# Square sums of five norms and the forget gate's running sum: fp32r products of two halves in place of fp32 products

## The chip, the cores and the metric

The kernel runs on one core of one Trainium2 chip. The metric is the time of the whole program on the device, in microseconds (us). Five engines work side by side, each through its own list of instructions in the order of the program: TensorE (PE, matrix products; PEld are its weight loads), VectorE (DVE), ScalarE (ACT), GpSimd (POOL) and SyncE (SP, which here only starts transfers). An instruction waits until what it reads has been written and what it overwrites has been read; whatever stands behind it on the same engine waits with it.

## The reference, cut to what matters

A decoder trunk of two layers on 256 tokens of width 1024. Every layer is a SwiGLU feed-forward (ffn), a token mixer (attention A in layer 0, attention B with forget gates in layer 1) and a second ffn. An RMS norm stands ahead of each of them and ahead of the shared keys and values:

```python
def rms_norm(x, g):
    xf = x.astype(jnp.float32)
    y = xf * lax.rsqrt(jnp.mean(xf * xf, axis=-1, keepdims=True) + EPS)
    return (y * g.astype(jnp.float32)).astype(x.dtype)
...
    log_f = jax.nn.log_sigmoid((h @ fgate_w + fgate_b).astype(jnp.float32))
    F = jnp.cumsum(log_f, axis=1)
```

## The kernel before

Activations lie transposed: `x` is eight tiles (chunks k = 0 to 7) of 128 features x 256 tokens. Every large product is split in three fp32r products: weight and activation are each kept as a high half (`wh`, `HH`, `hidh`) and a low half (`wl`, `HL`, `hidl`), and `mm3` forms high x high, low x high and high x low.

**Weights.** They come as 348 pieces `raw` (mostly 128 x 1024 fp32), six buffers deep. For each piece ACT makes `wh` (a cast, `cp_part`) and DVE makes `wl` (`raw` minus `wh`, `sub_part`), always in the order of the pieces. When `wl` of piece p has been made, SP starts the load of piece p+6 into the buffer that comes free. In an ffn's up-projection a unit j (256 gate and 256 up columns) takes four pieces, two chunks k each: the first piece serves k = 0 and 1 of the unit, the second k = 2 and 3, and so on, with 24 products for a piece.

**Order.** The class `InOrder` wraps each engine and keeps an estimated time `t` for it. Between the instructions that are written out, `bg`, `fill_act` and `fill_dve` put casts, subtractions and `ada_block`s (a 128 x 1024 multiply-and-sum on DVE that makes modulation columns) where these estimates leave room. A product whose second operand is F32 counts four times in PE's estimate. Inside `plain(f)` nothing is filled in. So each instruction that is added, and each product whose type changes, moves later fillings.

**Norms.** `x_update(n, ...)` (L438) runs once per chunk n: DVE adds the gated result to `x[n]`, ACT writes `HH` (x times the scale) and the squares `sq`, and the deferred `second()` writes `HL` on DVE and adds `sq` into `acc` (on POOL for n < 7 in the two attention outputs, else on DVE). `rstd_of` (L457) sums `acc` over the 128 partitions with one fp32 product against `ones` (1/1024 everywhere) into `psn`, ACT takes the reciprocal root `r0`, and three DVE instructions on `ra` refine it. The norm is taken late: the first products of the next stage run on the unnormed `HH`, `HL` (tiles `lp`, or `lg` and `lu`), and `psn` stands among them, after 24 of them in `late_pairs` and after 36 in `ffn(..., "late", ...)`. `MakeH` then makes the normed halves chunk by chunk: `ht` (DVE), `HH` (ACT), `HL` (DVE). There are five such norms: after ffn 0 and before attention A; after attention A and before ffn(0,1); before the shared keys and values; before attention B; after attention B and before ffn(1,1). The first norm of the program takes its squares another way (`sqs`, `parts`).

**Forget gate.** `lf` (16 x 256) is turned by two PE transposes into `plf`, ACT copies it to `lft`, and two fp32 products with the triangle `ub` (inside the constants tile `tri`) give the running sum `pFk`.

Of the kernel before, what the change touches and what calls it, by code (L numbers as in the profile page):

```python
# [10 lines left out]
F32 = mybir.dt.float32  # L11
F32R = mybir.dt.float32r
BF16 = mybir.dt.bfloat16
AF = mybir.ActivationFunctionType
ALU = mybir.AluOpType
PSUM = bass.MemoryType.PSUM

P = 128
D = 1024
S = 256  # L20
NC = D // P
HD = 64
AH = 8
BH = 16
# [80 lines left out]
def trunk(ctx, tc, a, out):  # L105
# [3 lines left out]
    act = InOrder(tc, nc.scalar, 0.13, 1 / 1200)  # L109
    dve = InOrder(tc, nc.vector, 0.08, 1 / 960)  # L110
    sp = InOrder(tc, nc.sync, 0.0, 1 / 704)
    cp_ = ctx.enter_context(tc.tile_pool(name="cp", bufs=1))
# [3 lines left out]
    kp = ctx.enter_context(tc.tile_pool(name="kp", bufs=2))  # L116
# [8 lines left out]
    def abank(name):  # L125
        return pp.tile([P, 512], F32, tag="ta", name=name)
# [4 lines left out]
    mm = pe.matmul  # L131

    def plain(f, *args):

        r = []
        act.plainly(lambda: dve.plainly(lambda: r.append(f(*args))))
        return r[0]
# [7 lines left out]
    for k in range(0, NC, 4):  # L145
        sp.dma_start(xx[:, k:k + 4], a["x"][:, k:k + 4])
    x = [xx[:, k] for k in range(NC)]
    ones = cp_.tile([P, P], F32, name="ones")
    dve.memset(ones, 1.0 / D)
    eps = cp_.tile([P, 1], F32, name="eps")  # L150
    dve.memset(eps, EPS)
# [13 lines left out]
    def table(func):  # L165
        act.preload_act_table(func)
# [66 lines left out]
    def need(*ms):  # L233
        while ada_done[0] < 2 * max(ada_at[m] for m in ms):
            credit[0] -= 1
            dve.plainly(ada_block)
# [163 lines left out]
    def run_laters():  # L400
        for e in list(laters):
            e[0] -= 1
            if e[0] <= 0:
                laters.remove(e)
                e[1]()

    def later(n, f):
        laters.append([n, f])
# [18 lines left out]
    acc = [None]  # L427

    def shift_cols(nxt):
# [2 lines left out]
        act.copy(HH[:, :, S:SX], shb)  # L432
        dve.tensor_tensor(HL[:, :, S:SX], shb, HH[:, :, S:SX].bitcast(F32), op=ALU.subtract)

    def x_update(n, ps, gate, nxt, acc_eng):

        dve.scalar_tensor_tensor(x[n], ps, gate[:, n:n + 1], x[n], op0=ALU.mult, op1=ALU.add)
        hh, hl = hn[n]  # L440
        A = mods[nxt[0]][1]
        act.activation(hh, x[n], AF.Copy, scale=A[:, n:n + 1])
        sq = kp.tile([P, S], F32, tag="sq", name=f"sq{n}")
        act.activation(sq, x[n], AF.Square)

        def second():
            dve.scalar_tensor_tensor(hl, x[n], A[:, n:n + 1], hh.bitcast(F32),
                                     op0=ALU.mult, op1=ALU.subtract)
            if n == 0:
                acc[0] = sq  # L450
            else:
                t = kp.tile([P, S], F32, tag="acc", name="acc", bufs=1) if n == 1 else acc[0]
                (acc_eng if n < NC - 1 else dve).tensor_tensor(t, acc[0], sq, op=ALU.add)
                acc[0] = t
        return second

    def rstd_of(then=None, parts=None):  # L457
        ps = abank("psn")[:, :S]
        parts = parts or [acc[0]]
        for i, p in enumerate(parts):  # L460
            mm(ps, ones, p, start=i == 0, stop=i == len(parts) - 1)
        r0 = kp.tile([P, S], F32, tag="r0", name="r0", bufs=1)
        act.activation(r0, ps, AF.Abs_reciprocal_sqrt, bias=eps)
        if then is not None:
            table(then)
        ra = kp.tile([P, S], F32, tag="ra", name="ra", bufs=1)
        dve.scalar_tensor_tensor(ra, ps, eps, r0, op0=ALU.add, op1=ALU.mult)
        dve.scalar_tensor_tensor(ra, ra, -0.5, r0, op0=ALU.mult, op1=ALU.mult)
        dve.scalar_tensor_tensor(r0, ra, 1.5, r0, op0=ALU.add, op1=ALU.mult)
        return r0  # L470
# [93 lines left out]
    def ffn(l, i, kind, m, nxt, at=2):  # L564
# [120 lines left out]
        for n in range(NC):  # L685
# [22 lines left out]
            def upd(n=n, po=po):  # L708
                f = x_update(n, po, mods[gate][1], nxt, dve)
                later(1, f)  # L710
# [167 lines left out]
    def v_proj(src, dst):  # L878

        for nh in range(2):  # L880
            banks = [mmbank(f"pv{t}") for t in range(2)]
            for kh in range(2):
                blk = take(src)
                for kk in range(4):
                    k = kh * 4 + kk
                    wh, wl = blk(kk * 512, 512)
                    hh, hl = hn[k]
                    for t in range(2):
                        ts = slice(t * P, t * P + P)
                        mm(banks[t], hh[:, ts], wh, start=k == 0, stop=False)  # L890
                        mm(banks[t], hh[:, ts], wl, start=False, stop=False)
                        mm(banks[t], hl[:, ts], wh, start=False, stop=k == NC - 1)
                        work(256)
                    if k == NC - 1:
                        for t in range(2):
                            act.copy(dst[t][nh], banks[t])
                    yield kk, 4
# [39 lines left out]
    for k in range(0, NC, 2):  # L937
        sq = kp.tile([P, 512], F32, tag="w512a" if k % 4 else "w512b", name=f"sqs{k}")
        act.activation(sq, xx[:, k:k + 2].rearrange("p a b -> p (a b)"), AF.Square)
        sq4.append(sq)  # L940
        if k % 4:
            i = k // 4
# [4 lines left out]
    ada_block()  # L947
    ada_block()
    rstd = rstd_of(None, [sq4[i][:, h * S:(h + 1) * S] for i in (0, 2) for h in range(2)])
    warm(6)  # L950
    pb = sbank("pb")[:AH, :UW]
# [5 lines left out]
    late = {}  # L957

    def constants():
        o = P + 2 * S  # L960
        raw = ap_.tile([P, 2, D], F32, tag="ada", name="misc").rearrange("p a b -> p (a b)")
        sp.dma_start(raw[:, :a["misc"].shape[1]], a["misc"])
        tri = cp_.tile([P, o], F32R, name="tri")
        late["mask"] = tri[:, 2 * P:P + S].bitcast(F32)
        late["ident"], late["ub"] = tri[:, :P].bitcast(F32), tri[:, P + S:].bitcast(F32)
        base = o

        def bias():
            act.copy(tri, raw[:, :base])
            table_ = kp.tile([AH, UW], F32, tag="w512b", name="table_")  # L970
            dve.tensor_copy(table_, ut)
            udram = tc.dram_tile([AH, UW], F32, name="udram")
            nc.gpsimd.dma_start(udram, table_)
            skew = tc.dram_tile([AH, P, UW], F32, name="skew")
            for hd in range(AH):
                nc.gpsimd.dma_start(skew[hd], bass.AP(udram.tensor, udram.offset + hd * UW, [[0, P], [1, UW]]))
            late["skew"] = skew

            ls = small[:, :2]
            lj = kp.tile([P, HD], F32, tag="w512a", name="lj")  # L980
            for i in range(2):
                q = o + 2 * i * HD
                dve.tensor_tensor_reduce(lj, raw[:, q:q + HD], raw[:, q + HD:q + 2 * HD], 1.0, 0.0,
                                         ALU.mult, ALU.add, accum_out=ls[:, i:i + 1])
            act.activation(ls, ls, AF.Exp)
            nlam = small[:, 2:3]
            dve.scalar_tensor_tensor(nlam, ls[:, 1:2], -LAMBDA_INIT, ls[:, 0:1],
                                     op0=ALU.add, op1=ALU.subtract)
            subg = small[:, 8:9]
            dve.tensor_scalar_mul(subg, vecs[:, V_SUB:V_SUB + 1], 1.0 - LAMBDA_INIT)  # L990
            late["nlam"], late["subg"] = nlam, subg
        later(10, bias)
# [6 lines left out]
    ident, mask, ub, skew, nlam, subg = (  # L999
        late[n] for n in ("ident", "mask", "ub", "skew", "nlam", "subg"))  # L1000
# [176 lines left out]
    op, rest = attention_a()  # L1177
# [40 lines left out]
    for i, (kk, n) in enumerate(v_proj("wkv", vb)):  # L1218
        if mh:
            mh.go()  # L1220
        run_laters()
        if i == 5:
            plf = abank("plf")
            for t in range(2):
                pe.transpose(plf[:, t * BH:(t + 1) * BH], lf[:, t * P:(t + 1) * P], ident[:BH, :BH])
            lft = kp.tile([P, 2 * BH], F32, tag="lft", name="lft", bufs=1)
            act.copy(lft, plf[:, :2 * BH])
        if i == 7:
            pFk = abank("pFk")
            mm(pFk[:BH, P:S], lft[:, BH:], ub[:, :P], start=True, stop=False, skip_group_check=True)  # L1230
            mm(pFk[:BH, :S], lft[:, :BH], ub, start=False, stop=True, skip_group_check=True)
            fk = kp.tile([BH, S], F32, tag="w512b", name="fk")
            act.activation(fk, pFk[:BH, :S], AF.Copy, scale=-1.0)

            fdram = tc.dram_tile([BH, P + S], F32, name="fdram")
            nc.gpsimd.dma_start(fdram[:, :P], fk[:, :P])
            nc.gpsimd.dma_start(fdram[:, P:], fk)
        if i == 8:
            need(*nm_)
            table(AF.Silu)  # L1240
            mh = MakeH(rstd, nm_)
            mh.go()
# [147 lines left out]
    op, rest = attention_b()  # L1390
# [130 lines left out]
```

## Time and profile before

| | |
|---|---|
| median of 3 runs | 968.13 us (968.04 to 970.2) |
| the profiled execution | 968.25 us, its span 966.5 us |
| PE busy | 957.2 us (99%) |
| DVE busy | 819.6 us (85%) |
| ACT busy | 558.7 us (58%) |
| granted TensorE clock | 0.999 of full |

The span is what the profile's rows cover; the time of the same execution is 1.75 us longer. In a timeline a row reads: start, duration, engine, line, operation, output<-inputs, shape, and in brackets how long the engine had been idle and what ended that. Matmuls are pipelined: a row's duration is longer than the step to the next row's start, and the step is what a product costs. Since the wrapper issues every instruction, nearly all rows carry its line, L100, and are told apart by tiles.

### The profile page before, as it was taken

What the parts mean: (1) busy time and instruction counts of PE and PEld (TensorE: products, weight loads), DVE (VectorE), ACT (ScalarE), POOL (GpSimd) and SP (SyncE); (2) the same over time, 40 slices, a digit from 0 to 9 for tenths busy, and PEclk for the clock granted to TensorE, in tenths of its full rate; (3) what the DMA queues carried; (4) which work ended last, traced back from release to release, by engine and by line L of the source; (5) the groups of instructions that cost most, each with busy time, mean ns of one, the idle gap of its engine ahead of it and who ended that gap; (6) DMA issues with size and microseconds to landing.
All of it is one profiled execution on the core that took longest, in us unless ns stands there. A gap on an engine that the chain in (4) does not pass through costs nothing.

```text
span 966.5 us, 20431 instructions
## 1 busy us (share of the span) xinstructions
PE 957.2 (99%) x8076; PEld 931.4 (96%) x8076; DVE 819.6 (85%) x1364; ACT 558.7 (58%) x911; POOL 68.6 (7%) x110
## 2 busy tenths in 40 slices
PE   9999999999999999999999999999999999999997
PEld 7999999998999999999997999999998899999997
DVE  6989978889999999878889989989988799555575
ACT  6575545576787745455576545445568676554432
POOL 0000200000112000000000000000053014300000
PEclk9999999999999999999999999999999999999999
DMA  9998999968767699888959799988895337977651
GB/s 357 414 369 293 346 385 332 327 216 282 288 206 261 204 364 387 309 291 311 327 178 379 292 340 340 353 302 317 318 313 158 115 120 223 269 163 258 189 150 44
DMA packets 69518, 267.87 MB, mean 277 GB/s; under 512 B 9429, under 2 KB 10270, under 8 KB 59311
## 3 DMA queue, kind: packets, MB, share of 16 engines
q1 hardware_dynamic: 66060, 259.35, 76.3%
q0 software_dynamic: 3072, 6.92, 2.5%
q8 instruction: 63, 1.03, 0.4%
q10 hardware_dynamic: 290, 0.32, 0.1%
q14 instruction: 33, 0.26, 0.1%
HBM read 264.41 MB, written 2.66 MB: 276 GB/s over the span
## 4 chain that ended last, share of the span: by engine, by line
PE 97%; DVE 1%; ACT 1%; issue 0%; POOL 0%; ACTq 0%
PE po L100 25%; PE pg L100 21%; PE pu L100 21%; PE pv L100 5%; PE pf L100 5%; PE lp L100 4%; PE pqk L100 3%; PE pw L100 3%; PE lq L100 1%; PE lu L100 1%; PE lg L100 1%; PE pk L100 1%; PE wb L100 1%; PE sb L100 1%; PE s L100 1%; DVE ada L100 1%
## 5 line engine op out<-in xcount | busy, mean ns | idle before, releaser
L100 ACT CAST wh<-raw 128x1024 fp32r<-128x1024 f32 (+1 forms) x360 | 347.8, 975 | 221.5 <-PE pu L100 77.2
L100 DVE TENSOR_TENSOR wl<-raw,wh 128x1024 fp32r<-128x1024 f32 (+1 forms) x360 | 400.6, 1132 | 70.2 <-ACT sg L100 20.6
L100 DVE CUSTOM_DVE_ANT_0 ada<-ada,cact,vecs 128x1024 f32<-128x1024 f32 x160 | 203.2, 1281 | 0.4 <-DMA ada<-in_ada 0.4
L100 PE MATMUL pg<-HH,wl 128*128 128x256 f32 x608 | 168.2, 277 | 0.0
L100 PE MATMUL pu<-HH,wh 128*128 128x256 f32 x608 | 168.1, 277 | 0.0
L100 PE MATMUL pg<-HL,wh 128*128 128x256 f32 x608 | 168.1, 277 | 0.0
L100 PE MATMUL pu<-HH,wl 128*128 128x256 f32 x608 | 168.1, 276 | 0.0
L100 PE MATMUL pu<-HL,wh 128*128 128x256 f32 x608 | 168.1, 276 | 0.0
L100 PE MATMUL pg<-HH,wh 128*128 128x256 f32 x608 | 168.1, 276 | 0.0
L100 PE MATMUL po<-hidh,wh 128*128 128x256 f32 x528 | 145.9, 276 | 0.0
L100 PE MATMUL po<-hidl,wh 128*128 128x256 f32 x528 | 145.9, 276 | 0.0
L100 PE MATMUL po<-hidh,wl 128*128 128x256 f32 x528 | 145.9, 276 | 0.0
L100 PEld LDWEIGHTS pg<-HH,wl 128*128 128x128 f32 x608 | 114.2, 188 | 0.1
L100 PEld LDWEIGHTS pg<-HH,wh 128*128 128x128 f32 x608 | 114.2, 188 | 0.0
L100 PEld LDWEIGHTS pu<-HH,wh 128*128 128x128 f32 x608 | 114.2, 188 | 0.0
L100 PEld LDWEIGHTS pg<-HL,wh 128*128 128x128 f32 x608 | 114.2, 188 | 0.0
L100 PEld LDWEIGHTS pu<-HL,wh 128*128 128x128 f32 x608 | 114.2, 188 | 0.0
L100 PEld LDWEIGHTS pu<-HH,wl 128*128 128x128 f32 x608 | 114.2, 188 | 0.0
L100 PEld LDWEIGHTS po<-hidh,wh 128*128 128x128 f32 x528 | 99.2, 188 | 0.0
L100 PEld LDWEIGHTS po<-hidh,wl 128*128 128x128 f32 x528 | 99.1, 188 | 0.0
L100 PEld LDWEIGHTS po<-hidl,wh 128*128 128x128 f32 x528 | 99.1, 188 | 0.0
L100 ACT CAST hidh<-hf 128x512 fp32r<-128x512 f32 x44 | 27.3, 621 | 42.0 <-DVE hf L100 42.0
(228 smaller groups left out, 1857.6 us busy)
## 6 DMA issues: line engine op xcount, KB each, us to landing
raw<-in_win SPq DMA_DIRECT2D x176, 512.0 KB, 6.8
ada<-in_ada SPq DMA_DIRECT2D x79, 1024.0 KB, 7.5
raw<-in_wout SPq DMA_DIRECT2D x48, 384.0 KB, 5.5
raw<-in_wout SPq DMA_DIRECT2D x48, 320.0 KB, 5.3
raw<-in_wqk SPq DMA_DIRECT2D x16, 512.0 KB, 5.1
raw<-in_wo SPq DMA_DIRECT2D x16, 512.0 KB, 5.4
raw<-in_wlast SPq DMA_DIRECT2D x16, 512.0 KB, 4.0
raw<-in_wv SPq DMA_DIRECT2D x8, 512.0 KB, 7.0
```

Of the source, the lines that this page charges most:

```text
L100: return self.tc.keep_in_program_order(f(*args, **kw))
```

## The change

In each of the five norms the finished sum `acc` is split, right after its last addition: ACT copies it to fp32r (`acc_sq` in the order's rows, a buffer of the tag that the squares use) and DVE subtracts that copy from `acc` (`acc_ht`, a buffer of the tag that `ht` uses). Two fp32r products with the same `ones` replace the one fp32 product. The first norm keeps its fp32 products. For the forget gate, `lft` becomes fp32r with twice the columns: ACT writes the high half, one more DVE instruction the low half, and the products with `ub` are done for both.

```diff
-    ones = cp_.tile([P, P], F32, name="ones")
+    ones_r = cp_.tile([P, P], F32R, name="ones")
+    ones = ones_r.bitcast(F32)
...
+    def halves(t):
+
+        h, l = (kp.tile([P, S], F32R, tag=tag, name=f"acc_{tag}") for tag in ("sq", "ht"))
+        act.copy(h, t)
+        dve.tensor_tensor(l, t, h.bitcast(F32), op=ALU.subtract)
+        return h, l
...
-                acc[0] = t
+                acc[0] = t if n < NC - 1 else plain(halves, t)
...
-        parts = parts or [acc[0]]
+        w = ones if parts else ones_r
+        parts = parts or acc[0]
         for i, p in enumerate(parts):
-            mm(ps, ones, p, start=i == 0, stop=i == len(parts) - 1)
+            mm(ps, w, p, start=i == 0, stop=i == len(parts) - 1)
...
-            lft = kp.tile([P, 2 * BH], F32, tag="lft", name="lft", bufs=1)
-            act.copy(lft, plf[:, :2 * BH])
+            lft = kp.tile([P, 4 * BH], F32R, tag="lft", name="lft", bufs=1)
+            act.copy(lft[:, :2 * BH], plf[:, :2 * BH])
+            dve.tensor_tensor(lft[:, 2 * BH:], plf[:, :2 * BH], lft[:, :2 * BH].bitcast(F32), op=ALU.subtract)
...
-            mm(pFk[:BH, P:S], lft[:, BH:], ub[:, :P], start=True, stop=False, skip_group_check=True)
-            mm(pFk[:BH, :S], lft[:, :BH], ub, start=False, stop=True, skip_group_check=True)
+            for o in (BH, 3 * BH):
+                mm(pFk[:BH, P:S], lft[:, o:o + BH], ub[:, :P], start=o == BH, stop=False, skip_group_check=True)
+            for o in (0, 2 * BH):
+                mm(pFk[:BH, :S], lft[:, o:o + BH], ub, start=False, stop=o > 0, skip_group_check=True)
```

The order of the instructions moves as well. The first place is the norm between attention A and ffn(0,1), on DVE. Before, from the last addition into `acc` (the three `wl` in one row are pieces 110 to 112 of the weights, the single `wl` is piece 113):

```order
L100 TENSOR_TENSOR acc<-acc,sq_4010 128x256
L100 TENSOR_TENSOR wl<-raw,wh 128x1024 x3
L100 SCALAR_TENSOR_TENSOR ra<-psn,eps,r_4076 128x256
L100 SCALAR_TENSOR_TENSOR ra<-ra,r_4076 128x256
L100 SCALAR_TENSOR_TENSOR r_4076<-ra,r_4076 128x256
L100 SCALAR_TENSOR_TENSOR ht_4095<-x,modall,r_4076 128x256
L100 SCALAR_TENSOR_TENSOR ht_4098<-x,modall,r_4076 128x256
L100 SCALAR_TENSOR_TENSOR HL<-ht_4095,modall,HH 128x256
L100 TENSOR_TENSOR wl<-raw,wh 128x1024
L100 SCALAR_TENSOR_TENSOR ht_4120<-x,modall,r_4076 128x256
L100 SCALAR_TENSOR_TENSOR HL<-ht_4098,modall,HH 128x256
```

Now, the end of the same stretch (ahead of it stand, without another piece, the new `acc_ht` between `acc` and the three `wl`, then `ra` to `r` and the chunks 0 to 4 of `ht`); the first `wl` here is piece 113, the second piece 114, the `ht` ahead of the first one belongs to chunk 6:

```order
L100 SCALAR_TENSOR_TENSOR ht_4148<-x,modall,r_4082 128x256
L100 SCALAR_TENSOR_TENSOR HL<-ht_4144,modall,HH 128x256
L100 SCALAR_TENSOR_TENSOR ht_4166<-x,modall,r_4082 128x256
L100 SCALAR_TENSOR_TENSOR HL<-ht_4148,modall,HH 128x256
L100 TENSOR_TENSOR wl<-raw,wh 128x1024
L100 SCALAR_TENSOR_TENSOR ht_4186<-x,modall,r_4082 128x256
L100 SCALAR_TENSOR_TENSOR HL<-ht_4166,modall,HH 128x256
L100 SCALAR_TENSOR_TENSOR HL<-ht_4186,modall,HH 128x256
L100 TENSOR_TENSOR wl<-raw,wh 128x1024
L100 TENSOR_TENSOR lt_4230<-lg_4025,r_4082 128x256
```

Piece 113 stood behind the first `HL` and stands behind the sixth now, five `ht` and five `HL` later; before, it was piece 114 that stood at that place, and piece 114 now follows the last `HL`. The norm between attention B and ffn(1,1) has the same move, with pieces 297 and 298.

The second place is ACT at the same norm, from the last squares; before:

```order
L100 ACTIVATE sq_4010<-x 128x256
L100 CAST wh<-raw 128x1024 x3
L100 ACTIVATE r_4076<-psn,eps 128x256
L100 ACT_TABLE_LOAD
L100 ACTIVATE HH<-ht_4095,modall 128x256
L100 ACTIVATE HH<-ht_4098,modall 128x256
L100 CAST wh<-raw 128x1024
```

and now:

```order
L100 ACTIVATE sq_4015<-x 128x256
L100 CAST acc_sq<-acc 128x256
L100 CAST wh<-raw 128x1024 x3
L100 ACTIVATE r_4082<-psn,eps 128x256
L100 ACT_TABLE_LOAD
L100 ACTIVATE HH<-ht_4105,modall 128x256
L100 ACTIVATE HH<-ht_4108,modall 128x256
L100 ACTIVATE HH<-ht_4124,modall 128x256
```

The cast of the sum stands ahead of three casts of weights (pieces 111 to 113), and the fourth cast (piece 114) has gone behind the sixth `HH`.

The third place is the forget gate, on PE. Before:

```order
L100 MATMUL pv_6730<-wl,HH 128x512
L100 MATMUL pv_6730<-wh,HL 128x512
L100 MATMUL pFk<-tri,lft 16x128
L100 MATMUL pFk<-tri,lft 16x256
L100 MATMUL pv_6831<-wh,HH 128x512
```

and now:

```order
L100 MATMUL pv_6745<-wl,HH 128x512
L100 MATMUL pv_6745<-wh,HL 128x512
L100 MATMUL pFk<-tri,lft 16x128 x2
L100 MATMUL pFk<-tri,lft 16x256 x2
L100 MATMUL pv_6846<-wh,HH 128x512
```

Each fp32 product has become two fp32r products at the same place. The same holds for `psn` in the five norms, which stands where it stood. The rest of PE's order is what it was. In the middles of ffn(0,1) and ffn(1,0), DVE's `ada_block`s and `wl` change places by one here and there.

More of the change, by code (lines that the diff above doesn't have):

```diff
@@ L964, in constants @@
         late["mask"] = tri[:, 2 * P:P + S].bitcast(F32)
-        late["ident"], late["ub"] = tri[:, :P].bitcast(F32), tri[:, P + S:].bitcast(F32)
+        late["ident"], late["ub"] = tri[:, :P].bitcast(F32), tri[:, P + S:]
         base = o
```

## The prediction

> **What bounds the kernel now.** I read the page's busy times first, then the chain of work that ended last, then PE's own waits.
>
> ```profile
> PE 957.2 (99%) x8076; PEld 931.4 (96%) x8076; DVE 819.6 (85%) x1364; ACT 558.7 (58%) x911; POOL 68.6 (7%) x110
> ...
> PE 97%; DVE 1%; ACT 1%; issue 0%; POOL 0%; ACTq 0%
> ...
> PE wa L100 <- issue: 0.4, 1, 0.4
> ```
>
> PE makes 97% of the chain, and after the start its longest wait is this 0.4 us. So what PE saves is saved, and what PE newly waits is lost: later stages have no slack that would give it back. DVE, at 85%, runs only a little ahead of PE in places, and these places decide.
>
> **The products, one by one.** PE's timeline at the first of the five norms:
>
> ```profile
> 197.81 0.59 PE L100 MATMUL psn<-acc,ones 128*128 128x256 f32 x2
> 198.06 0.47 PE L100 MATMUL lp<-HH,wh 128*128 128x258 f32 x1
> 198.37 0.28 PE L100 MATMUL lp<-HH,wl 128*128 128x258 f32 x1
> 198.49 0.28 PE L100 MATMUL lp<-HL,wh 128*128 128x258 f32 x1
> ```
>
> From `psn` to the second ordinary product pass 0.56 us (198.37 - 197.81). Of this 0.12 belong to the one `lp` between (the step from 198.37 to 198.49), so the fp32 product costs 0.44. What an fp32r product of 256 columns costs stands at unit 1 of ffn(0,1):
>
> ```profile
> 315.07 0.28 PE L100 MATMUL pg<-HH,wl 128*128 128x256 f32 x1
> ...
> 317.80 0.28 PE L100 MATMUL pg<-HH,wl 128*128 128x256 f32 x1
> ...
> 320.52 0.28 PE L100 MATMUL pg<-HH,wl 128*128 128x256 f32 x1
> ```
>
> 24 products lie from one row to the next: 2.72 / 24 = 0.113 us each (a step of 2.73 in the first pair). Two of them cost 0.23, so a norm saves up to 0.21; I count 0.20.
>
> The forget gate:
>
> ```profile
> 519.88 0.39 PE L100 MATMUL pv<-wl,HH 128*128 128x512 f32 x1
> 520.11 0.40 PE L100 MATMUL pv<-wh,HL 128*128 128x512 f32 x1
> 520.43 0.82 PE L100 MATMUL pFk<-tri,lft 128*16 128x128 f32 x4
> ...
> 521.52 0.39 PE L100 MATMUL pv<-wl,HH 128*128 128x512 f32 x1
> ```
>
> Two `pv` steps (0.23 each, as from 519.88 to 520.11) taken from 521.52 - 520.11 leave 0.95 us for `pFk` and the change-over on both sides. Four fp32r products take at least 2 x 0.113 + 2 x 0.057 = 0.34, if 128 columns cost half of 256. At most they cost the 0.95 of now. I take 0.53, the streaming time plus about 0.19 of change-over as now (520.43 comes 0.09 after the `pv` step ends, 0.10 more lie behind), since the shapes stay: a saving of 0.42, between 0 and 0.6. The new DVE subtraction on 128 x 32 has 2 us until `pFk`, and is hidden.
>
> **The chain that is added.** Each norm now has a cast on ACT and a subtraction on DVE between the last addition and the second `psn` product. No row shows the cast; its nearest rows (ACT, 128 x 256) are 0.41 for the squares and 0.47 for `r`, which reads PSUM:
>
> ```profile
> 305.33 0.41 ACT L100 ACTIVATE sq<-x 128x256 f32<-128x256 f32 x1
> 305.64 2.94 ACT L100 CAST wh<-raw 128x1024 fp32r<-128x1024 f32 x3
> 308.48 0.47 ACT L100 ACTIVATE r<-psn,eps 128x256 f32<-128x256 f32 x1
> ```
>
> I take 0.40, since the cast reads and writes the same memory as the squares; 0.47 is the upper end, and nothing here is shorter than the 0.31 by which 305.64 follows 305.33. The subtraction is the operation and shape of the `acc` row (0.41). A hand-over from engine to engine takes 0.03 to 0.04: `r` below ends at 198.92 and `ra`, which waited for it, starts at 198.95.
>
> At the first norm (and alike at the third and fourth, behind an ffn) the rows are:
>
> ```profile
> 198.45 0.47 ACT L100 ACTIVATE r<-psn,eps 128x256 f32<-128x256 f32 x1 [1.05 <-PE psn L100]
> ...
> 196.59 0.42 DVE L100 TENSOR_TENSOR acc<-acc,sq 128x256 f32<-128x256 f32 x1
> ...
> 198.95 0.48 DVE L100 SCALAR_TENSOR_TENSOR ra<-psn,eps,r 128x256 f32<-128x256 f32 x1 [0.81 <-ACT r L100]
> ```
>
> `acc` ends at 197.01, the cast at 197.45, the subtraction at 197.91. The low half's product could start at 197.92 (197.81 + 0.113): it waits 0.03. What is pushed back behind it is one cast on ACT, where 1.05 us were idle, and one `wl` on DVE, where 0.81 were. So these three norms save 0.17 each, **0.51** in all; with the longer cast 0.10 each.
>
> **The second norm, ahead of ffn(0,1), has less room.** DVE and PE there:
>
> ```profile
> 306.17 0.41 DVE L100 TENSOR_TENSOR acc<-acc,sq 128x256 f32<-128x256 f32 x1
> 306.51 3.48 DVE L100 TENSOR_TENSOR wl<-raw,wh 128x1024 fp32r<-128x1024 f32 x3
> 309.92 0.48 DVE L100 SCALAR_TENSOR_TENSOR ra<-psn,eps,r 128x256 f32<-128x256 f32 x1
> ...
> 312.41 0.49 DVE L100 SCALAR_TENSOR_TENSOR HL<-ht,modall,HH 128x256 fp32r<-128x256 f32 x1 [0.18 <-ACT HH L100]
> 312.81 1.22 DVE L100 TENSOR_TENSOR wl<-raw,wh 128x1024 fp32r<-128x1024 f32 x1
> 313.95 0.48 DVE L100 SCALAR_TENSOR_TENSOR ht<-x,modall,r 128x256 f32<-128x256 f32 x1
> ...
> 318.01 0.48 DVE L100 SCALAR_TENSOR_TENSOR HL<-ht,modall,HH 128x256 fp32r<-128x256 f32 x1
> 318.41 1.22 DVE L100 TENSOR_TENSOR wl<-raw,wh 128x1024 fp32r<-128x1024 f32 x1
> ...
> 320.69 0.48 DVE L100 SCALAR_TENSOR_TENSOR HL<-ht,modall,HH 128x256 fp32r<-128x256 f32 x1 [0.26 <-ACT HH L100]
> ...
> 307.27 0.59 PE L100 MATMUL psn<-acc,ones 128*128 128x256 f32 x2
> ```
>
> `acc` ends at 306.58; cast 306.62 to 307.02; subtraction 307.06 to 307.47; the low product at 307.51 instead of 307.38. Here a norm saves only **0.07**.
>
> Behind the subtraction DVE goes on with the three `wl` at 307.40 instead of 306.51 (a next instruction starts 0.34 after this shape, as 306.51 does after 306.17): 0.89 late. ACT's three casts start 0.31 after the new one, at 306.93, and `r` 1.29 late, ending at 310.24; DVE needs it at 310.81 (309.92 + 0.89), so `r` does not add. The first `HL` then stands at 313.30.
>
> Now the moved piece. Piece 113 is the row at 312.81, and unit 1 of the ffn needs it for its chunks 2 and 3: PE uses it first at 317.80 (the unit's first `wl` product is the row at 315.07, and 24 products later the second piece is due). There were 3.8 us to spare (it ends at 314.03). In the new order it stands behind the sixth `HL`. That `HL` moves by the 0.89 and, since `ht` now follows the first `HL` after 0.40 (as 318.41 follows 318.01) where it followed after 1.54 (313.95 - 312.41), back by 1.14: 318.01 + 0.89 - 1.14 = 317.76. Piece 113 runs from 318.16 to 319.38 and is there at 319.42. PE arrives at 317.73: it waits **1.69 us**. Nothing hides this, since PE's products keep their order and the next one all need later chunks.
>
> The piece behind it (114) follows the last `HL`: as 320.69 stands 2.28 behind 318.41, it starts at 318.16 + 2.28 + 0.40 = 320.84 and is there at 322.10. PE, after 24 more products, wants it at 322.14: just in time. Piece 115 was just late before:
>
> ```profile
> 323.12 0.28 PE L100 MATMUL pg<-HH,wh 128*128 128x256 f32 x1
> 323.29 0.39 PE L100 MATMUL pg<-HH,wl 128*128 128x256 f32 x1
> 323.51 0.29 PE L100 MATMUL pg<-HL,wh 128*128 128x256 f32 x1
> ```
>
> These two steps take 0.39 instead of 0.23. With PE 1.6 later this **0.16** goes.
>
> **The fifth norm, ahead of ffn(1,1),** has the same move with pieces 297 and 298:
>
> ```profile
> 781.35 0.41 DVE L100 TENSOR_TENSOR acc<-acc,sq 128x256 f32<-128x256 f32 x1
> 781.68 3.48 DVE L100 TENSOR_TENSOR wl<-raw,wh 128x1024 fp32r<-128x1024 f32 x3
> ...
> 787.58 0.49 DVE L100 SCALAR_TENSOR_TENSOR HL<-ht,modall,HH 128x256 fp32r<-128x256 f32 x1 [0.18 <-ACT HH L100]
> ...
> 783.00 0.59 PE L100 MATMUL psn<-acc,ones 128*128 128x256 f32 x2
> ...
> 793.53 0.28 PE L100 MATMUL pg<-HH,wl 128*128 128x256 f32 x1
> ```
>
> `acc` ends at 781.76, the halves are there at 782.69, `psn` is due at 783.00: no wait, **0.20** saved. The three `wl` start at 782.58, 0.90 late, and the first `HL` at 788.48. The sixth follows 4.46 later (317.76 - 313.30), at 792.94, piece 297 runs from 793.34 to 794.56 and is there at 794.60. PE arrives at 793.33: it waits **1.27 us**.
>
> **The sum.** Saved: 0.51 + 0.07 + 0.20 + 0.42 + 0.16 = 1.36. Lost: 1.69 + 1.27 = 2.96. Net +1.6 us on the profiled execution's 968.25 us (0.12 above the median of the runs shown, 968.13): **969.8 us**. A cast of 0.47 would add 0.07 at both waits and cost another 0.07 in four of the norms: 970.2. Hand-overs and steps that are better by a tenth at each end give 969.2. Within 0.3% (2.9 us) a measurement of this kernel cannot tell a time from no change.
>
> **The rivals.**
> - *No wait:* the moved pieces arrive in time, for instance because DVE takes the pairs of `ht` and `HL` faster once no piece stands among them (0.91 us a pair now, 0.80 if they followed each other at 0.40). For it: six pairs at 0.80 would bring half a microsecond. Against it: to win 1.69 they would have to go at about 0.6, and two DVE instructions need 0.80. Then only the saving of the products stays: 968.25 - 1.2 = 967.0.
> - *PE's clock falls in the waits*, the case that ends clearly slower. At the program's start the clock is low, and the fp32 product shows it:
>
> ```profile
> L100 PE MATMUL psn<-acc,ones x10: 377/378/378, 197.8 to 783.2; 128*128 128x256 f32 x10
> L100 PE MATMUL psn<-sqs,ones x8: 634/634/635, 7.5 to 10.5; 128*128 128x256 f32 x8
> ```
>
>   If an idle PE falls back to that state and stays in it for some 10 us of work, as at the start (rows of 634 ns still at 10.5), each place loses about 5 us: 975 with one, 980 with both. It decides from the length of the idle time that the clock bears. The trace shows that 0.4 us do nothing (the wait quoted first; the page grants full clock after it); 1.7 it does not show. The Trainium skill ("TensorE: Matmul & The Clock Gate", Part 1) states that the clock halves after an idle window of about 3.4 us and returns after as long a busy one; by that neither wait is long enough, and a fall would cost about 1.7 us each, an estimate from that page. No run here shows the window.
> - *The halves are no cheaper:* if the pair of products costs PE the 0.44 of one fp32 product, and `pFk` its 0.95, the waits alone stay: 968.25 + 2.8 = 971.0. The `pg` rows speak against it, with the same tile shapes.
>
> **How the numbers follow.** The forecast has 0.72, no wait (or most of it hidden) 0.14, no cheaper halves 0.06, the clock 0.03; 0.05 stay for later loads that follow the late `wl` (SP starts the load of piece p+6 when `wl` of p is made) and for what I do not see. The range leaves out the clock and part of the rest: 966.9 to 971.2. Slower by over 0.3%: the clock, half of the third rival, and half of the unseen, 0.09. Faster by over 0.3% would need twice the whole saving: 0.02. Within: 0.89.
>
> **What would show it.** In the new trace `psn` should be two rows whose steps are 0.11 to 0.12; PE should wait once for `wl` behind the second norm (1.7 us, 84 products after `psn`) and once behind the fifth (1.3 us), each time with DVE busy on `ht` and `HL`; all else on PE should be shifted, not stretched. No such wait proves the moved piece harmless and this forecast wrong; a wait for `HL` or for the casts would put the cause elsewhere; a wait at `psn` of over 0.3 us would mean that the cast or the hand-over is mis-sized.

## The result and the profile after

The changed kernel takes **973.25 us** (median of 8 runs, 972.29 to 978.53) against 968.64 us (8 runs of before, 968.04 to 970.2): a ratio of **1.0057** [1.0037, 1.0078], slower by 4.6 us. The forecast was 969.8, with 971.2 as the upper end. The eight times fall in two groups, five from 972.3 to 973.3 and three from 977.4 to 978.5; the profiled execution (977.4 us, span 975.6) belongs to the second. Later runs profiled both.

The page of after, busy times and the chain of work by engine:

```profile
PE 963.1 (99%) x8076; PEld 937.0 (96%) x8076; DVE 822.7 (84%) x1370; ACT 561.7 (58%) x916; POOL 70.4 (7%) x110
...
PE 94%; DVE 3%; ACT 1%; DMA 1%; issue 0%; POOL 0%; ACTq 0%
```

Its waits of PE (total us, times, longest):

```profile
PE pg L100 <- DVE wl L100: 2.6, 2, 1.4
...
PE lp L100 <- ACT HH L100: 0.2, 1, 0.2
```

The two waits of PE for `wl` that the forecast named are there, and DVE's share of the chain has grown from 1% to 3%. But PE is also *busy* 5.9 us longer, although each fp32 product became two cheaper ones. That was not foreseen.

**The waits.** Timelines of after at the second norm, DVE and then PE (start, duration):

```profile
306.99 0.42 DVE L100 TENSOR_TENSOR acc_ht<-acc,acc_sq 128x256 fp32r<-128x256 f32 x1 [0.47 <-ACT acc_sq L100]
307.33 3.49 DVE L100 TENSOR_TENSOR wl<-raw,wh 128x1024 fp32r<-128x1024 f32 x3
...
313.24 0.48 DVE L100 SCALAR_TENSOR_TENSOR HL<-ht,modall,HH 128x256 fp32r<-128x256 f32 x1 [0.18 <-ACT HH L100]
...
317.82 0.48 DVE L100 SCALAR_TENSOR_TENSOR HL<-ht,modall,HH 128x256 fp32r<-128x256 f32 x1
318.22 1.22 DVE L100 TENSOR_TENSOR wl<-raw,wh 128x1024 fp32r<-128x1024 f32 x1
```

```profile
307.20 0.28 PE L100 MATMUL psn<-acc_sq,ones 128*128 128x256 f32 x1
307.47 0.38 PE L100 MATMUL psn<-acc_ht,ones 128*128 128x256 f32 x1
307.69 0.29 PE L100 MATMUL lg<-HH,wh 128*128 128x258 f32 x1
...
315.06 0.28 PE L100 MATMUL pg<-HH,wl 128*128 128x256 f32 x1
...
316.47 0.28 PE L100 MATMUL pg<-HH,wl 128*128 128x256 f32 x1
...
319.49 0.39 PE L100 MATMUL pg<-HH,wl 128*128 128x256 f32 x1 [1.45 <-DVE wl L100]
```

The low half comes 0.27 behind the high one (307.20 to 307.47), a wait of some 0.15 for the subtraction, and from there to the next product it takes 0.22 (307.69) instead of 0.12. So the pair costs 0.49 us here, more than the 0.44 of the fp32 product. The cast and the subtraction put the three `wl` at 307.33 (forecast 307.40), the sixth `HL` stands at 317.82 (forecast 317.76), and piece 113 is there at 319.44 (forecast 319.42). The rows show 1.45 us of PE idle; counted in steps, as the forecast did, the wait is 1.6. Again the product that waited takes about twice its step, 0.23 (to 319.72). Behind every wait of PE for `wl` shown below this step is 0.22 to 0.23, and the forecast had no term for it.

**The pace.** From 315.06 to 316.47 lie 12 products: 1.41 / 12 = 0.118 us each, where before took 0.113. Nothing is waited for in between. This goes on to the end of ffn(0,1). The view by stretches, PE alone, over the same 110 us of the three profiles (start:end, length, PE busy and number of products, granted clock, DMA share, GB/s); before, after, and after run once more (after_again, below):

```profile
330.00:440.00 110.00, 110.00 (x973) 1.00 0.90 330
```

```profile
330.00:440.00 110.00, 110.00 (x937) 1.00 0.89 314
```

```profile
330.00:440.00 110.00, 110.00 (x972) 1.00 0.92 326
```

PE is busy throughout and its granted clock is full in all three, but after finishes 36 products fewer. One starts every 0.117 us instead of 0.113 (110 / 937 and 110 / 973). Compared product by product with before, after loses 6.2 us in this way: it is 1.81 us behind right after the wait (319.72 against 317.91) and 8.01 at the last product of the ffn (491.81 against 483.80). In after_again the same kernel has the pace of before there: that makes the two groups of times.

### The profile page after: what moved, and what is told of

It is laid out like the page before. It is cut to its first block, busy times and chain, and to the rows that moved or that the text cites. A ratio compares the mean times of both kernels' runs of the same rounds, so it can differ in the third digit from the quotient of the medians.

```text
span 975.6 us, 20434 instructions
## 1 busy us (share of the span) xinstructions
PE 963.1 (99%) x8076; PEld 937.0 (96%) x8076; DVE 822.7 (84%) x1370; ACT 561.7 (58%) x916; POOL 70.4 (7%) x110
## 3 DMA queue, kind: packets, MB, share of 16 engines
q8 instruction: 63, 1.03, 0.4%
## 4 chain that ended last, share of the span: by engine, by line
PE 94%; DVE 3%; ACT 1%; DMA 1%; issue 0%; POOL 0%; ACTq 0%
PE po L100 24%; PE pg L100 21%; PE pu L100 21%; PE pv L100 5%; PE pf L100 5%; PE lp L100 4%; PE pqk L100 3%; PE pw L100 3%; PE lq L100 1%; PE pk L100 1%; DVE HL L100 1%; DMA raw<-in_wkk 1%; DVE wl L100 1%; PE wb L100 1%; PE sb L100 1%; PE s L100 1%
## 5 line engine op out<-in xcount | busy, mean ns | idle before, releaser
L100 PE MATMUL po<-wh,hidh 128*128 128x256 f32 x176 | 48.6, 276 | 0.0
```

The source lines that it names most:

```text
L100: return self.tc.keep_in_program_order(f(*args, **kw))
```

## The experiments

Rows of one set (a letter for the chip, a number for the set) ran on the same chip beside the same runs of before. "Near 975" counts executions of 974.9 us or more.

| set | run | median us (runs) | before | ratio [95%] | near 975 |
|---|---|---|---|---|---|
| A1 | after_again | 972.67 (5) | 968.91 | 1.0040 [1.0028, 1.0052] | 0 |
| A1 | neutral | 969.36 (11) | 968.91 | 1.0011 [0.9991, 1.0031] | 2 |
| A1 | order_only | 971.62 (5) | 968.91 | 1.0035 [1.0023, 1.0047] | 0 |
| A1 | second_only | 975.33 (12) | 968.91 | 1.0041 [1.0023, 1.0060] | 7 |
| A2 | no_second | 969.25 (11) | 968.68 | 1.0003 [0.9995, 1.0012] | 0 |
| A2 | first_three | 968.25 (11) | 968.68 | 0.9992 [0.9981, 1.0004] | 0 |
| A2 | wait_only | 970.16 (11) | 968.68 | 1.0014 [1.0004, 1.0024] | 0 |
| A2 | second_noshift | 970.24 (12) | 968.68 | 1.0029 [1.0006, 1.0053] | 5 |
| B3 | set_back_2 | 970.13 (11) | 968.90 | 1.0013 [1.0004, 1.0022] | 0 |
| B3 | wait_one | 969.61 (11) | 968.90 | 1.0003 [0.9994, 1.0012] | 0 |
| B3 | gate_only | 968.62 (10) | 968.90 | 0.9998 [0.9989, 1.0007] | 0 |
| C4 | second_reset | 970.03 (11) | 968.56 | 1.0015 [1.0006, 1.0024] | 0 |
| C5 | second_only_b | 970.48 (11) | 968.66 | 1.0013 [1.0003, 1.0022] | 0 |
| C5 | second_reset_b | 970.17 (12) | 968.66 | 1.0011 [1.0003, 1.0020] | 0 |
| C5 | wait_one_b | 969.61 (11) | 968.66 | 1.0005 [0.9996, 1.0014] | 0 |

### Order against work: after_again, neutral, order_only, set_back_2

after_again is the changed kernel itself.

> The changed kernel once more. Its eight times so far fall in two groups, 972.3 to 973.3 and 977.4 to 978.5 us, and the profiled one is of the second: there PE waits 1.6 and 1.3 us for the moved pieces, and in all of ffn(0,1) a piece of 24 products takes 2.83 us instead of 2.72, which makes 6.2 us. If that slow pace is a state that an execution falls into or not, a profile of the first group shows the two waits again and the slow pace in a part of ffn(0,1) or nowhere; times again in two groups, 5 us apart. If the two groups come from something else (a transfer, a wait), a profile of the first group shows 2.83 us too. The moved pieces alone would give 968.6 + 1.6 = 970.2, less than any time so far.

neutral keeps every edit, but sets the planner's clocks back behind each one, so that everything else keeps the order of before:

```diff
-                acc[0] = t if n < NC - 1 else plain(halves, t)
...
+                    was = act.t, dve.t
+                    acc[0] = plain(halves, t)
+                    act.t, dve.t = was
...
+        if w is ones_r:
+            pe.t += 2 * S / 2350
```

> The whole change, with the planner's clocks set back after each new instruction, so that every instruction of before stands in the order of before and the new ones are only put in. The moved pieces as cause of the two waits: no wait for wl behind the second and fifth norm, and 2.9 us less than the changed kernel in the same pace: 967.4 with the pace of before, about 973.6 with the slow pace in ffn(0,1). If the halves themselves set the slow pace, it shows here too; if the moved order sets it, 2.72 us a piece and 967.4. Rival to the waits' cause (the cast and subtraction are late, not the order): the waits stay at over 1 us each.

order_only is the reverse: before's instructions and products, with the estimates of after, so in the order of after without the inserted instructions:

```diff
                 acc[0] = t
+                if n == NC - 1:
+                    at = max(act.t, InOrder.ready[(t.tensor.name, 0)]) + act.fixed + act.rate * S
+                    act.t = at
+                    dve.t = max(dve.t, at + 0.06) + dve.fixed + dve.rate * S
...
+        if len(parts) == 1:
+            pe.t -= 2 * S / 2350
```

> The products of before (one fp32 product a norm, fp32 forget gate, no halves) in the order of the changed kernel: pieces 113 and 297 stand behind the sixth HL. By the working of the prediction, with DVE 0.9 us earlier than with the halves: piece 113 is there at 318.5, a wait of about 0.7 us, piece 297 at 793.75, about 0.2 us; 969.0 to 969.5 us in the pace of before. If the order sets the slow pace, ffn(0,1) takes 2.83 us a piece and the time is about 975; if the halves set it, 2.72 us.

set_back_2 is the whole change with the clocks set back behind norm 2 alone (`if nth[0] in BACK`, BACK = 2):

> The whole change; the planner's clocks are set back behind the halves of norm 2 alone, so that ffn(0,1) has the order of before (piece 113 not moved, the loads of raw and ada not exchanged), while piece 297 behind norm 5 is moved as in the whole change. Theory F (it is the replanning behind norm 2 that costs, through the wait at piece 113 and at the end of ffn(0,1)): 969.4 of the whole change in before's order + 1.33 - 0.35 for the other wait behind norm 5 = 970.4; no wait at 113, 0.8 at 115, 1.3 at 297, none over 0.2 at the end of ffn(0,1). Theory G (the work that the halves add costs, whatever the order): 972 to 973.

Set against their own runs of before: the whole change +3.8 us, the order alone +2.7, the edits in before's order +0.5, and the whole change with ffn(0,1) in before's order +1.2. So about 2.5 us (3.8 - 1.2) hang on what the planner does behind norm 2. Some 0.8 (1.2 - 0.5) would be left for what it does behind norm 5, but that is within the intervals of the two ratios. The edits themselves, for which the forecast had a gain of over 1 us, are not shown to gain anything. The rest is read from the traces.

after_again, PE's timeline at pieces 113 and 297 and at the end of ffn(0,1):

```profile
320.01 0.38 PE L100 MATMUL pg<-HH,wl 128*128 128x256 f32 x1 [1.54 <-DVE wl L100]
...
486.38 0.39 PE L100 MATMUL lp<-HH,wh 128*128 128x258 f32 x1 [0.16 <-ACT HH L100]
...
796.96 0.39 PE L100 MATMUL pg<-HH,wl 128*128 128x256 f32 x1 [1.17 <-DVE wl L100]
```

The same three places in order_only:

```profile
318.72 0.39 PE L100 MATMUL pg<-HH,wl 128*128 128x256 f32 x1 [0.74 <-DVE wl L100]
...
486.03 0.39 PE L100 MATMUL lp<-HH,wh 128*128 128x258 f32 x1 [1.08 <-ACT HH L100]
...
796.78 0.39 PE L100 MATMUL pg<-HH,wl 128*128 128x256 f32 x1 [0.21 <-DVE wl L100]
```

The moved pieces alone cost 0.74 and 0.21 of PE's idle time; with the added cast and subtraction they cost 1.54 and 1.17. This part went as forecast. The middle row is **a third wait**, of which the forecast knew nothing. The chain of waits of after, at that place, shows where it comes from (start, us, what):

```profile
482.11 8.91 DMA raw<-in_wkk
...
491.12 1.05 ACT wh L100
492.17 0.12 ACT HH L100
492.28 0.04 issue
492.33 0.76 PE lp L100 x4
```

A load of `raw` lands late, the cast `wh` waits for it, the first `HH` stands behind that cast on ACT, and the first `lp` waits for `HH`. Before, that cast waited for PE and no load (it could start as soon as `po` released its buffer). ACT's rows, before and in after_again:

```profile
482.46 1.06 ACT L100 CAST wh<-raw 128x1024 fp32r<-128x1024 f32 x1 [0.98 <-PE po L100]
```

```profile
485.18 1.05 ACT L100 CAST wh<-raw 128x1024 fp32r<-128x1024 f32 x1 [0.61 <-DMA raw<-in_wkk]
```

set_back_2 has no wait at this place; its one long wait is the one behind norm 5:

```profile
796.70 0.38 PE L101 MATMUL pg<-HH,wl 128*128 128x256 f32 x1 [1.23 <-DVE wl L101]
```

So the late load belongs to the replanning behind norm 2, which also exchanges loads of `raw` and `ada` on SP: 68 places of SP's list differ from before in after and in order_only, none in set_back_2 and neutral. Which of the exchanged loads does it was not tried. In before's order the loss moves elsewhere. neutral, which has no wait at 113 and 297, waits at piece 115:

```profile
324.75 0.38 PE L100 MATMUL pg<-HH,wl 128*128 128x256 f32 x1 [0.59 <-DVE wl L100]
```

Piece 115 was just late before, so it has no room for DVE's 0.9 us of added lateness. 0.7 us are lost there against before, and 0.4 at piece 299.

### Which edits pay: no_second, first_three, gate_only

All three keep the order of before. no_second leaves norm 2 in fp32 (`SPLIT = (1, 3, 4, 5)`), first_three norms 2 and 5 (`SPLIT = (1, 3, 4)`), gate_only all norms:

```diff
+                elif nth[0] not in SPLIT:
+                    acc[0] = [t]
...
-        w = ones if parts else ones_r
+        w = ones if parts or nth[0] not in SPLIT else ones_r
```

> Halves in the norms 1, 3, 4 and 5 and in the gate, norm 2 as before, everything in the order of before. Theory A (the loss of the whole change in before's order is the wait that norm 2 puts ahead of piece 115, and the slow pace that can follow it): no wait at piece 115, no slow pace in ffn(0,1), savings of 0.12 + 0.19 + 0.1 + 0.2 us at the norms and 0.4 at the gate against a wait of 0.35 at piece 299, so about 968.0 against 968.7 of before, and next to none of the executions near 975. Theory B (the cheaper products and their added work cost time wherever they stand): 969.4 as with all five norms, and about one in five executions near 975.

> Halves in the norms 1, 3 and 4 and in the gate; norms 2 and 5, behind which a piece's low half is almost late, as before; order of before. Theory A: no new wait at pieces 115 and 299; 0.12 + 0.19 + 0.1 us saved at the norms and 0.4 at the gate, so about 967.9 against 968.7. Theory B: 968.7 or more.

> Halves in the forget gate alone, all norms as before, order of before. The four products of pFk take 0.6 us less than the two of before, and the products behind them 0.2 us more if their slower rhythm comes from the gate: 968.3 against 968.7. If that rhythm has another origin: 968.1.

The wait at piece 115 is gone in no_second, but its time (969.25) is that of theory B. In its trace 0.4 us are lost at piece 299, 0.25 at the end of ffn(0,1), and pieces 112 to 115 run at 0.118. An earlier wait of 0.7 us for `hidl` at 143 us, ahead of every edit, is that execution's own. first_three, at 968.25, keeps the savings of norms 1, 3 and 4 and of the gate and has none of the new waits at 115, 297 and 299. Its ratio, 0.9992 [0.9981, 1.0004], is not told apart from 1, and neither is that of gate_only. No version that was run is shown to beat the kernel before.

The gate does what it should. gate_only's PE rows, against the 0.95 us worked out for before:

```profile
520.42 0.40 PE L101 MATMUL pv<-wh,HL 128*128 128x512 f32 x1
520.65 0.51 PE L101 MATMUL pFk<-tri,lft 128*16 128x128 f32 x4
521.00 0.39 PE L101 MATMUL pv<-wh,HH 128*128 128x512 f32 x1
```

From the end of the `pv` step (520.42 + 0.23) to the next `pv` pass 0.35 us: the 0.34 of the pure streaming estimate, with no change-over. So the 0.19 of change-over belonged to the fp32 products, and the saving is 0.60. The `pv` products behind them keep their rhythm here, so the 0.2 us that they lose in after_again has another origin.

### What sets the pace: second_only, wait_only, wait_one, second_noshift, second_reset

For these runs one more thing of the kernel must be known. A few pieces have their `wh` and `wl` written 16 columns further into the buffers (the table `shift`). In the up-projections these are pieces 5, 11 and 20 in ffn 0 and one piece in each later ffn, in ffn(0,1) piece 116. They are called shifted.

second_only has halves at norm 2 alone (`SPLIT = (2,)`), an fp32 gate and before's order:

> Halves in the second norm alone (attention A to ffn(0,1)), in the order of before, all else as before. The prediction's working gives no wait for wl and 0.07 us saved: 968.5 us. If the two short products in place of the fp32 product set PE's slow pace in the stage behind them, 2.83 us a piece in ffn(0,1) and about 974.7; if pace is a matter of chance in any kernel, groups of times as in the changed kernel, whatever the edit.

Seven of its twelve executions were near 975, so the slow pace comes with norm 2 changed alone. PE's timeline in one of them at piece 115 (all `pg<-HH,wl` products behind the wait, to 326.60):

```profile
324.73 0.39 PE L101 MATMUL pg<-HH,wl 128*128 128x256 f32 x1 [0.59 <-DVE wl L101]
325.19 0.28 PE L101 MATMUL pg<-HH,wl 128*128 128x256 f32 x1
326.25 0.28 PE L101 MATMUL pg<-HH,wl 128*128 128x256 f32 x1
326.60 0.28 PE L101 MATMUL pg<-HH,wl 128*128 128x256 f32 x1
```

Nine products lie between 325.19 and 326.25: 0.118 each, from the end of the wait on; ahead of it they took 0.113. Is it the wait, or the norm's new pair of products? wait_only has before's products and, at norm 2, a cast and two subtractions that nothing reads; wait_one has one subtraction:

```diff
         act.copy(h, t)
-        dve.tensor_tensor(l, t, h.bitcast(F32), op=ALU.subtract)
-        return h, l
+        for _ in range(2):
+            dve.tensor_tensor(l, t, h.bitcast(F32), op=ALU.subtract)
+        return [t]
```

> The products of before in the order of before; at norm 2 one cast on ScalarE and two subtractions on VectorE are added whose results nothing reads. Theory C (a short wait of PE inside the stage is enough to set which of the two paces PE takes afterwards): a wait of 0.5 to 1 us at piece 115, and between a third and two thirds of the executions near 975 to 976 with products of 0.118 us from there to the end of ffn(0,1); the others near 969.5. Theory D (the second product of the norm, of another kind, sets the pace): the same wait, 969.5, and no more executions near 975 than before has (2 of 23).

> As in the run wait_only, with one subtraction in place of two that nothing reads. Theory C (the end of any wait of PE draws the pace anew): a single wait of 0.2 to 0.5 us at piece 115 and the time of before + 0.3, 969.0, in most executions, with at least two of eleven near 975. Theory D (the pace is slow only where norm 2 has its pair of products): 969.0 and no more executions near 975 than before has.

wait_only got two waits, at pieces 114 and 115:

```profile
322.47 0.39 PE L101 MATMUL pg<-HH,wl 128*128 128x256 f32 x1 [0.35 <-DVE wl L101]
322.93 0.28 PE L101 MATMUL pg<-HH,wl 128*128 128x256 f32 x1
323.99 0.28 PE L101 MATMUL pg<-HH,wl 128*128 128x256 f32 x1
324.34 0.28 PE L101 MATMUL pg<-HH,wl 128*128 128x256 f32 x1
326.07 0.39 PE L101 MATMUL pg<-HH,wl 128*128 128x256 f32 x1 [0.51 <-DVE wl L101]
326.53 0.28 PE L101 MATMUL pg<-HH,wl 128*128 128x256 f32 x1
327.56 0.28 PE L101 MATMUL pg<-HH,wl 128*128 128x256 f32 x1
```

After the first wait nine products take 1.06 us (322.93 to 323.99), 0.118 each; after the second 1.03 (326.53 to 327.56), 0.114. So the pace changed at both waits, once each way, without any change to the products. Over the executions, though, theory C's share did not come: none of eleven near 975, in wait_only (one at 973.9) as in wait_one. Theory D seemed to hold. second_noshift then takes second_only and leaves piece 116 unshifted:

```diff
-    for (l, i), j in ((0, 0), K0 + 1), ((0, 1), 2), ((1, 0), 0), ((1, 1), 2):
+    for (l, i), j in ((0, 0), K0 + 1), ((1, 0), 0), ((1, 1), 2):
```

> Halves at norm 2 alone, as in the run second_only, and piece 116 isn't shifted by 16 columns. Theory C (the wait sets the pace, and the shifted piece passes it on): the same two groups, near 969.2 and 975.3, each in a third to two thirds of the executions. Theory E (the shifted piece, whose products come in another rhythm, sets the pace): one group alone, or all of them in the pace that they have ahead of piece 116.

Five of twelve were near 975, in both groups as before: the shifted piece is not what brings the slow pace (theory E falls). second_reset adds six shifted pieces to second_only, to break the rhythm:

```diff
+    shift.update({p: 16 for p in range(124, 148, 4)})
```

> As in the run second_only, with six more pieces shifted by 16 columns inside ffn(0,1) (124, 128, 132, 136, 140, 144), each of which takes 2.84 us instead of 2.72: 0.7 us more in all, so 969.9 where the pace is fast. Theory H (every break of the rhythm draws the pace anew, slow products included): the slow executions lose it at one of the six, so they spread between 970.5 and 974.5 and hardly one is at 975.5 or above; the trace shows where. Theory I (a slow pace stays until the stage ends, whatever breaks the rhythm): two groups, near 969.9 and 976, as in second_only.

No execution was above 971.32. But this was another chip than second_only's, so the three kernels went side by side on one:

> The kernel of second_only once more, now on the same chip as the next two. If the slow pace belongs to the kernel: again a third to two thirds of the executions near 975.5, the others near 969.3. If it belongs to the chip on which it ran: another share, down to none, and the next two have the same.

> The kernel of second_reset once more. Theory H (breaks of the rhythm draw the pace anew): no execution near 976 even where second_only_b has several, the slow ones spread between 970.5 and 974.5. Theory I (only the chip differed): as many near 976 as second_only_b has near 975.5.

> The kernel of wait_one once more. Theory C (the end of a wait draws the pace, whatever the products): as many executions near 975.5 as second_only_b has. Theory D (tied to the pair of products at norm 2): none or one near 975.5, the others at 969.5, even where second_only_b has several.

second_only, with seven of twelve near 975 on one chip, has none of eleven on this one. The share goes with the chip as much as with the kernel, so the times can't tell H and I apart. Theory D, that the pace is slow only where norm 2 has its pair, falls as it stands: in 9 of the 17 profiles, after_again, wait_only and first_three among them, PE has the slow pace over several unshifted pieces of ffn 0, ahead of every edit, and gate_only and no_second begin unit 1 of ffn(0,1) with it. That the pair makes a slow ffn(0,1) more likely is neither shown nor refuted. On chip A the kernels with the pair at norm 2 were near 975 in 14 of 40 executions (after_again, neutral, second_only, second_noshift), and those without it in none of 38 (order_only, no_second, first_three, wait_only); but the kernel before, which has no pair either, had two beside them (975.65 and 975.1 us, not profiled). On chips B and C neither kind was.

What ends a slow pace can be read from the profiles. The shifted pieces of the up-projections are slow in all of them. Here are PE's rows of before at the start of pieces 299, 300 (the shifted one of ffn(1,1)) and 301:

```profile
798.86 0.28 PE L100 MATMUL pg<-HH,wh 128*128 128x256 f32 x1
...
801.58 0.28 PE L100 MATMUL pg<-HH,wh 128*128 128x256 f32 x1
...
804.42 0.28 PE L100 MATMUL pg<-HH,wh 128*128 128x256 f32 x1
```

Piece 299 takes 2.72 us, the shifted piece 2.84 (0.118 a product). In second_only_b, at the start of pieces 10, 11 (shifted), 12 and 13 of ffn 0:

```profile
42.70 0.28 PE L101 MATMUL pf<-HH,wh 128*128 128x256 f32 x1
...
45.53 0.27 PE L101 MATMUL pf<-HH,wh 128*128 128x256 f32 x1
...
48.38 0.28 PE L101 MATMUL pf<-HH,wh 128*128 128x256 f32 x1
...
51.10 0.28 PE L101 MATMUL pf<-HH,wh 128*128 128x256 f32 x1
```

Piece 10 is slow (2.83), the shifted piece 11 too (2.85), piece 12 has the fast 2.72. Over all profiles, in ffn 0, ffn(0,1) and ffn(1,1), PE came slow into a shifted piece 15 times; 12 times it was fast behind it, three times (after and second_only at piece 116, wait_only at piece 11) it stayed slow. So a shifted piece mostly ends a slow pace, as theory H has it for a break of the rhythm, but not always.

Shown is that the slow pace exists, that in the places followed here it starts where PE resumes after a wait or begins a stage, that a shifted piece can end it, and what it costs. **What decides which pace PE takes stays open.**

## Why the prediction was wrong

The step that failed is the last sentence on the trace: "all else on PE should be shifted, not stretched". With it the sum had two losing terms and no others, and only 0.05 of chance was left for anything else. The terms, as after_again shows them against before (how far the same products lag between two places of the two traces; after_again took 971.76 us, 3.5 more than before's profiled execution):

| term | forecast us | measured us |
|---|---|---|
| norms 1, 3 and 4 | -0.51 | -0.43 |
| norm 2 | -0.07 | +0.04 |
| norm 5 | -0.20 | -0.21 |
| `pFk` | -0.42 | -0.60 |
| piece 115 no longer late | -0.16 | -0.18 |
| wait at piece 113 | +1.69 | +1.82 |
| wait at piece 297 | +1.27 | +1.46 |
| wait at the end of ffn(0,1) | none | +0.43 |
| the same at the end of ffn(1,0) | none | +0.20 |
| stretches at another pace (attention A, `pv` behind `pFk`, attention B, ahead of piece 297), less 0.22 won back ahead of norm 2 | none | +0.65 |
| sum | +1.60 | +3.18 |

Another 0.38 us had come up ahead of norm 1, where nothing was changed: in ffn 0 five pieces ran at the slow pace (some 0.5 us, after a start that was a little faster).

- **The cheaper products: right in sum, and partly by luck.** 1.38 saved instead of 1.36. `pFk` was mis-sized: the change-over went with the fp32 products, and 0.18 more was saved. About as much was missed at the norms. In norms 1 and 2 the low half waits, as forecast, but the product that waited then takes 0.22 instead of 0.12: norm 1 saves 0.06 instead of 0.17, and norm 2 loses 0.04. Norms 3 and 4 have no wait there and save 0.19 and 0.18. The rival "the halves are no cheaper" falls.
- **The waits behind norms 2 and 5: right in cause and place.** They are 0.13 and 0.19 longer than forecast; 0.11 of each is the doubled step of the product that waited (320.01 to 320.23 and 796.96 to 797.18 in after_again).
- **"Later stages have no slack": not quite.** Before, PE waited 0.17 us for `x` at the start of ffn(0,1); after_again comes there later, does not wait, and wins 0.22 back.
- **The rival "no wait": falls**, since the pairs of `ht` and `HL` kept their 0.91 us.
- **The rival "PE's clock falls in the waits": falls as a cause, though its time nearly came.** The rows on the 110 us above have a granted clock of 1.00 behind a wait of 1.45 us. The Trainium skill's rule ("TensorE: Matmul & The Clock Gate", Part 1), that the clock needs a longer idle window to fall, agrees with that.
- **Everything else shifted, not stretched: wrong twice.** First, the planner replans a whole stage: it exchanged loads far behind the edit, and at the end of ffn(0,1) PE waits for one of them. The forecast followed two moved pieces in the order, not the loads; "later loads" stood there without a price. Second, PE's 0.113 us is one of two paces. The step was read from one stretch of one execution and used as a constant of the chip, though the shifted pieces of that same profile ran at 0.118. Three of the first eight executions took the other pace through a whole ffn, at some 6 us.

The exchanged loads, the short slow stretches and the unpriced step behind each wait, with the 0.38 of ffn 0, take after_again's profiled execution to 971.76, already above the range; the 0.5 to 1.6 us between it and the lower group (972.3 to 973.3) were not traced. The whole ffn at the slow pace gives the group at 977 to 978 and moves the median, 973.25, to the upper end of the lower group.

## What to carry to other kernels

When an order is planned from estimates, an edit is worth what it saves minus what the replanning moves, and this must be followed to the end of the stage: loads as well as the pieces next to the edit. Before a chain is lengthened, look up the least slack behind it in the old order (here piece 115, at none), since 0.9 us of lateness cost 0.7 us there though nothing moved. And run such a change in the old order, and the new order without the change: these two runs (+0.5 and +2.7 us) say which half to mend. A step read from a profile should be looked up in every stage and beside every irregular piece before it is used as a constant.

## What the runs showed of the hardware that was not expected

- The same stream of fp32r products of 256 columns, each with its own weight load, runs at **0.113 or at 0.118 us** a product at full granted clock, for a whole stage (some 175 us here, 6.2 us of loss). The Trainium skill ("TensorE: Matmul & The Clock Gate", Back-to-back issue gap) says that the spacing in such a stream is set by both the load and the product; by its formula for a product alone 256 columns at full clock would be 109 ns, an estimate. Both paces lie above that, and no run here shows what makes PE take one or the other.
- The pace changed at waits of under 1 us, in both directions (wait_only, both in one execution).
- Pieces of the up-projections whose weights lie 16 columns further into their buffer ran at 0.118 in every profile, and PE, slow ahead of such a piece, was fast behind it in 12 of 15 cases.
- A product that PE had to wait for takes about two steps, 0.22 to 0.23 us in place of 0.113 or 0.118 (at all the waits at pieces 113, 114, 115 and 297 and at the end of ffn(0,1) shown here). So each wait delays what follows by another 0.11 us.
- One kernel (second_only) had seven of twelve executions with the slow pace on one chip and none of eleven on another, while the kernel before, in the same two sets, had one such execution on the first and none on the second.
